# A hybrid GLA/MLA layer on one core: the two output-gate projections of GLA as one seven-product scheme on token tiles, between the two v projections

## The chip, the cores and the metric

The kernel runs on one core of a Trainium2 chip. The metric is the device time of one launch in microseconds (us). The kernel before takes 894.04 us, the median of three runs (893.48 to 894.49). One more execution was taken with the hardware profiler; every time below is from that one unless it is called a median of runs.

## The reference, cut to what matters

One decoder layer on 512 tokens with a model width of 1024, all in fp32. It has two sub-layers: token mixing (gated linear attention, GLA, and latent attention, MLA, side by side on the same normalised input, merged by gates) and a squared-ReLU MLP. The change touches the GLA branch.

```python
h = layer_norm(x, ln_in_g, ln_in_b)                      # 512 x 1024
q_g, k_g, v_g, r_g, a_lr, q_lat, kv_lat, gate_logits = split(h @ w_in)
log_a = log_sigmoid(a_lr @ w_gla_a2 + b_gla_a2) / 16     # decay of each key channel
o_gla = gla_chunked(q_g * 128 ** -0.5, k_g, v_g, log_a)  # 4 heads, dk 128, dv 256
o_gla = rms_norm(o_gla, gla_norm_g)                      # per head
y_gla = (o_gla * silu(r_g)) @ w_o_gla
y_mla = ...                                              # latent attention
g_gla, g_mla = split(sigmoid(gate_logits + b_gate))
mix = (g_gla * y_gla + g_mla * y_mla) @ w_out
```

`r_g` is 512 tokens x 1024 columns: 256 columns for each of four heads. Only `silu(r_g)` is used, and only by the last step of a head's output. The product that makes it, `h @ w_in[:, r]`, is what the change computes in another way.

## The kernel before: tiles, stages and who sets the order

**Products.** An fp32 product is made of three fp32r matmuls. `split` (L109) makes a high part on ACT (a copy) and a low part on DVE (a subtraction); the three matmuls are high by high, high by low and low by high, summed in PSUM. `hT` holds the normalised input as eight tiles of 128 channels x 512 tokens, each in a high and a low part.

**Weights.** `plan` (L144) puts pieces of 512 KB (two blocks of 128 rows x 512 columns) on a list, the stream. `pump` (L177) asks for the piece after next from DRAM (`fetch`, L163, on SP's queue, into one of three `wraw` buffers) and splits the next piece into `whi` on ACT (L189) and `wlo` on DVE (L190). `whi` and `wlo` have two buffers each.

**Two ways to lay out a product.** `gemm_fm` (L235) puts output columns on the partitions and tokens along the free axis. `gemm_tm` (L260) puts tokens on the partitions: for each of eight blocks of 128 rows and each of four token tiles it issues the three matmuls of L279 to L281, each 128x512, so that 512 output columns take 8 x 4 x 3 = 96 of them in four PSUM banks. v and r use `gemm_tm`, in two halves of 512 columns (two heads) each.

**Order of the work.** A Python program writes the instructions; each engine runs its own in a fixed order that is set when the program is built. Side work is written as generators ("lanes"). `tick` advances the first `WID` lanes by one step (to their next `yield`) from inside a product's loop, and `finish` drives a lane to its end at once. So where a `tick` stands decides between which matmuls a lane's instructions land; a scheduler at build time may still shift instructions of different lanes against each other.

The stages around the change, in time: the latents, q and k (k until about 93 us), then `proj_v(0)` (heads 0 and 1), `proj_r(0)`, `finish(t_lat2)`, `proj_v(1)` (heads 2 and 3), `proj_r(1)` (until about 225 us), then the first gate product g,0 and the seven-product units g0 and g1.

**Lanes that run there.** `lane_levels` runs `gla_levels` (L667) for head 0, 1, 2, 3. For each block size s from 2 to 256 POOL advances running sums of the decay (`advance`, L680 and L681), ACT takes exponentials (L686), DVE multiplies them with q and k (`M`, L688), PE makes the scores (L742), and DVE puts them into the score tile `SD` (L698, L733, L734), or splits them (s128, s256). `proj_v(1)` drives this lane through head 1 before it copies its results out. `lane_out` runs `gla_out` (L765) for each head once its scores, its v and its gate r are there: PE multiplies scores by v (L785 to L787), ACT squares and sums (L789, `osq`), DVE scales (L792, `gss`), POOL takes the power -0.5 (L794, `grs`), DVE multiplies by the gate (L799, `og`), PE transposes (L805).

`proj_r` copies each PSUM bank out by a tanh on ACT (L654, `th`) and two DVE operations (L658, `rg`).

**Sums of h.** The units g0 and g1 already use a seven-product scheme (a form of Winograd's and Strassen's) on 2 x 2 blocks of weight and input. They need sums of quarters of `hT`. `h_early` (L944) forms them on DVE (L949 to L956), splits them (128x512, `sh`) and stores them to DRAM (`hsd`), as a lane spawned after the q product; `h_load` (L1111) loads them again. `u_load` (L1031) forms a sum of weights by transfers alone: one load into a `wq` tile from SP's queue and one accumulating transfer onto it from POOL's (L1036). `unit` (L1038) calls `tick(3)` after every second of its four row blocks. After g0's product "t3" the program runs `finish(*t_gla)`.

## Time and profile before

| what | value |
|---|---|
| median of three runs | 894.04 us (893.48 to 894.49) |
| profiled execution | 894.09 us |
| its span on the core | 892.3 us |
| granted TensorE clock, mean | 0.997 |
| PE busy | 875.2 us, 98% |
| DVE busy | 619.0 us, 69% |
| ACT busy | 459.4 us, 51% |
| POOL busy | 168.0 us, 19% |
| DMA | 119.38 MB, mean 134 GB/s |

PE is the matrix engine, PEld its weight loads, DVE the vector engine, ACT the scalar engine, POOL the GpSimd engine; SP issues most of the transfers. A row of a timeline gives the start, the duration, the engine, the line of the kernel, the operation, output and inputs, and in brackets how long the engine stood idle before it and what ended that. A row of waits gives the waiting instruction, what ended its waits, the sum in us, how many, and the longest. A row of groups gives, after the bar, busy time and mean ns of one, and after the second bar the idle time before. Matmuls are pipelined: the duration of one (0.39 us for 128x512) overlaps the next.

### The profile page before, as it was taken

What the parts mean: (1) busy time and instruction counts of PE and PEld (TensorE: products, weight loads), DVE (VectorE), ACT (ScalarE), POOL (GpSimd) and SP (SyncE); (2) the same over time, 40 slices, a digit from 0 to 9 for tenths busy, and PEclk for the clock granted to TensorE, in tenths of its full rate; (3) what the DMA queues carried; (4) which work ended last, traced back from release to release, by engine and by line L of the source; (5) the groups of instructions that cost most, each with busy time, mean ns of one, the idle gap of its engine ahead of it and who ended that gap; (6) DMA issues with size and microseconds to landing.
All of it is one profiled execution on the core that took longest, in us unless ns stands there. A gap on an engine that the chain in (4) does not pass through costs nothing.

```text
span 892.3 us, 12880 instructions
## 1 busy us (share of the span) xinstructions
PE 875.2 (98%) x4868; PEld 762.5 (85%) x4868; DVE 619.0 (69%) x1002; ACT 459.4 (51%) x808; POOL 168.0 (19%) x192
## 2 busy tenths in 40 slices
PE   6999999999999999999999999999999999999996
PEld 5988888888899988888888888988888888889985
DVE  7838987568365745657756797887556646787865
ACT  6456554455365543445644424365457546656720
POOL 1003555436120010100000002003500520131000
PEclk9999999999999999999999999999999999999998
DMA  7416632212997423121207618005950990399312
GB/s 247 121 47 200 225 119 72 71 48 68 305 272 195 124 89 112 38 60 54 96 24 273 197 48 306 2 1 122 308 136 9 273 257 29 79 230 235 118 65 79
DMA packets 80254, 119.38 MB, mean 134 GB/s; under 512 B 8464, under 2 KB 46224, under 8 KB 80192
## 3 DMA queue, kind: packets, MB, share of 16 engines
q1 hardware_dynamic: 63680, 85.54, 30.0%
q0 software_dynamic: 14592, 29.37, 14.7%
q10 hardware_dynamic: 1920, 3.66, 1.1%
q8 instruction: 38, 0.62, 0.3%
q14 instruction: 24, 0.20, 0.1%
HBM read 97.04 MB, written 8.91 MB: 119 GB/s over the span
## 4 chain that ended last, share of the span: by engine, by line
PE 94%; DVE 3%; DMA 1%; issue 1%; ACT 0%; POOLq 0%; DVEq 0%
PE mm L245 12%; PE mm L247 12%; PE mm L246 12%; PE mm L279 7%; PE mm L280 7%; PE mm L281 7%; PE mm L1061 3%; PE mm L1060 3%; PE mm L1059 3%; PE px L1344 2%; PE px L1345 2%; PE px L1343 2%; PE mm L1344 2%; PE mm L1345 2%; PE mm L1343 2%; PE px L742 2%
## 5 line engine op out<-in xcount | busy, mean ns | idle before, releaser
L190 DVE TENSOR_TENSOR wlo<-wraw,whi 128x1024 fp32r<-128x1024 f32 (+2 forms) x95 | 105.4, 1109 | 108.4 <-ACT whi L189 103.9
L189 ACT ACTIVATE whi<-wraw 128x1024 fp32r<-128x1024 f32 (+2 forms) x95 | 90.7, 955 | 89.5 <-PE mm L246 36.6
L245 PE MATMUL mm<-h,whi 128*128 128x512 f32 x256 | 99.9, 391 | 0.0
L246 PE MATMUL mm<-h,whi 128*128 128x512 f32 x256 | 99.9, 390 | 0.0
L247 PE MATMUL mm<-h,wlo 128*128 128x512 f32 x256 | 95.5, 389 | 0.0
L1362 POOL DMA_DIRECT2D res<-ev x42 | 37.3, 1008 | 179.0 <-ACT ev L1360 154.7
L190 DVE TENSOR_TENSOR wlo<-wq,whi 128x1024 fp32r<-128x1024 f32 x36 | 44.1, 1225 | 27.0 <-ACT whi L189 26.8
L247 PEld LDWEIGHTS mm<-h,wlo 128*128 128x128 f32 x256 | 48.1, 188 | 10.0
L245 PEld LDWEIGHTS mm<-h,whi 128*128 128x128 f32 x256 | 48.1, 188 | 9.7
L246 PEld LDWEIGHTS mm<-h,whi 128*128 128x128 f32 x256 | 48.1, 188 | 9.6
L189 ACT ACTIVATE whi<-wq 128x1024 fp32r<-128x1024 f32 x36 | 38.1, 1058 | 26.2 <-PE mm L1060 14.3
L279 PE MATMUL mm<-whi,h 128*128 128x512 f32 x128 | 50.7, 409 | 0.0
L280 PE MATMUL mm<-wlo,h 128*128 128x512 f32 x128 | 50.5, 395 | 0.0
L281 PE MATMUL mm<-whi,h 128*128 128x512 f32 x128 | 50.2, 394 | 0.0
L1060 PE MATMUL mm<-sh,whi 128*128 128x256 f32 x160 | 45.3, 283 | 0.0
L1059 PE MATMUL mm<-sh,whi 128*128 128x256 f32 x160 | 45.3, 283 | 0.0
L1061 PE MATMUL mm<-sh,wlo 128*128 128x256 f32 x160 | 45.3, 283 | 0.0
L189 ACT ACTIVATE xh<-wraw 128x1024 fp32r<-128x1024 f32 (+1 forms) x28 | 27.4, 987 | 29.2 <-PE mm L281 15.9
L190 DVE TENSOR_TENSOR xl<-wraw,xh 128x1024 fp32r<-128x1024 f32 (+1 forms) x28 | 31.3, 1130 | 9.6 <-ACT xh L189 9.5
L686 ACT ACTIVATE E<-rp 128x256 f32<-128x256 f32 x64 | 26.1, 417 | 22.7 <-POOL rp L681 13.9
L1405 ACT ACTIVATE relu<-mm 128x512 f32<-128x512 f32 x24 | 14.1, 596 | 41.8 <-PE mm L247 41.8
L409 POOL TENSOR_TENSOR mv<-mv,mhalf 128x1 f32<-128x1 f32 x4 | 3.3, 837 | 170.3 <-DVE mv L408 170.3
(433 smaller groups left out, 2662.8 us busy)
## 6 DMA issues: line engine op xcount, KB each, us to landing
wraw<-in_w_ff_dram SPq DMA_DIRECT2D x36, 512.0 KB, 5.2
wraw<-in_w_in_dram SPq DMA_DIRECT2D x35, 512.0 KB, 3.5
wq<-in_w_ff_dram POOLq DMA_DIRECT2D x26, 512.0 KB, 9.5
res<-ev POOLq DMA_DIRECT2D x42, 256.0 KB, 9.8
wq<-in_w_in_dram SPq DMA_DIRECT2D x10, 512.0 KB, 5.5
hsd<-sh SPq DMA_DIRECT2D x16, 256.0 KB, 2.6
sh<-hsd SPq DMA_DIRECT2D x16, 256.0 KB, 5.3
wraw<-in_w_o_gla_dram SPq DMA_DIRECT2D x8, 512.0 KB, 3.7
```

The costliest lines, as they stand in the source:

```text
L189: st["ins"] = act(hi[:, :nk, :n], raw[:, :nk, :n], AF.Copy)
L190: st["lo"] = vtt(lo[:, :nk, :n], raw[:, :nk, :n], f(hi[:, :nk, :n]), op=ALU.subtract)
L245: mm(o, hi[:, c], xh, start=first, stop=False)
L246: mm(o, hi[:, c], xl, start=False, stop=False)
L247: mm(o, lo[:, c], xh, start=False, stop=last)
L279: mm(o, xh, hi[:, :n], start=opens, stop=False, skip_group_check=share)
L280: mm(o, xh, lo[:, :n], start=False, stop=False, skip_group_check=share)
L281: mm(o, xl, hi[:, :n], start=False, stop=last, skip_group_check=share)
L1059: mm(oa, hi[:, k, c], xh, start=opens and k == 0 and a == 0, stop=False, skip_group_check=True)
L1060: mm(oa, hi[:, k, c], xl, start=False, stop=False, skip_group_check=True)
L1061: mm(oa, lo[:, k, c], xh, start=False, stop=k == 3, skip_group_check=True)
L1362: nc.gpsimd.dma_start(res[tt + t][:, j * T:(j + 1) * T], e, accum_op=ALU.add)
```

## The change

Both halves of r become one product in seven parts. The 1024 rows of the weight are paired in blocks of 128 (even and odd), the 1024 columns are halves of 512, and the tokens are halves of 256. The seven products are, in this order, "11", "21", "t2", "t1", "t3", "22" and "t4". Each multiplies one weight block, or a sum of blocks, with one quarter of `hT`, or a sum of quarters, over four row blocks and two token tiles: 4 x 2 x 3 = 24 matmuls of 128x512. Products accumulate in the same PSUM bank where the scheme allows it; six banks are also copied to SBUF (`er`) and combined there by DVE. `silu` is the former evacuation.

The t weights are sums made by transfers: `r_prep`, a new lane, loads the block "12" three times (twice 512 KB each, SP's queue) and adds "11" or "22" to it by accumulating transfers from POOL's queue (t2 gets both); after the product "t1", `r_acc4` adds "21" onto t2's tile, which makes t4. The sums of `hT` come from `h_early`'s DRAM tiles, loaded by `x_load` from SP's queue. `h_early` therefore starts before q (after six empty steps), splits by 256 columns and stores four tiles for each pair of blocks; both lanes are finished before `proj_r`.

The order is now v for heads 0 and 1, all of r, v for heads 2 and 3. The gates of heads 2 and 3 are complete one product before those of heads 0 and 1, and `gla_out` waits until all four token tiles of its head's gate are there. In g0, the tick after the second row block is gone, and `finish(*t_gla)` follows "t4" in place of "t3".

```diff
@@ -302,15 +302,34 @@
         PL["lat", i] = plan("w_in", C_A + i * half, half, res=True)
     PL["q"] = plan("w_in", C_Q, T)
     PL["k"] = plan("w_in", C_K, T)
-    for hp in range(2):
-        PL["v", hp] = plan("w_in", C_V + hp * T, T)
-        PL["r", hp] = plan("w_in", C_R + hp * T, T)
+    WQ = {}
+
+    RY, RT, RA4 = 2, ((0, 0), (1, 0), (1, 1)), "t1"
+    RW = (("11", 0), ("21", 1), ("t2", 3), ("t1", 2), ("t3", 6), ("22", 5), ("t4", 4))
+
+    def r_src(op, hf):
+        i, j = int(op[0]) - 1, int(op[1]) - 1
+        c0 = C_R + j * T
+        return I["w_in"].rearrange("(k p) n -> p k n", p=P)[:, 4 * hf + i:4 * hf + i + 3:2, c0:c0 + T]
+
+    PL["v", 0] = plan("w_in", C_V, T)
+    PL["r"] = []
+    for op, _ in RW:
+        for hf in range(2):
+            PL["r"].append(len(stream))
+            e = {"nk": 2, "n": T, "res": False}
+            if op[0] == "t":
+                e["src"] = lambda q=("r", op, hf): WQ[q]
+            else:
+                e["dmas"] = [(slice(0, 2), r_src(op, hf), None)]
+            stream.append(e)
+    PL["v", 1] = plan("w_in", C_V + T, T)
+
...
@@ -646,18 +665,94 @@
...
-    def proj_r(hp):
-        hs = (2 * hp, 2 * hp + 1)
-
-        def e(a, j, ps):
-            th = B([P, T], F32, "th")
-            act(th, ps, AF.Tanh, scale=0.5)
-            for i, h in enumerate(hs):
-                if Rg[h] is None:
-                    Rg[h] = A([P, NT, HV], F32, "rg")
-                stt(Rg[h][:, a, :], th[:, i * HV:(i + 1) * HV], 1.0, ps[:, i * HV:(i + 1) * HV],
-                    op0=ALU.add, op1=ALU.mult)
-        gemm_tm([PL["r", hp]], hT, T, e, fine=3)
+    def silu(j, a, ps):
+        th = B([P, T], F32, "th")
+        act(th, ps, AF.Tanh, scale=0.5)
+        for i in range(2):
+            h = 2 * j + i
+            if Rg[h] is None:
+                Rg[h] = A([P, NT, HV], F32, "rg")
+            stt(Rg[h][:, a, :], th[:, i * HV:(i + 1) * HV], 1.0, ps[:, i * HV:(i + 1) * HV],
+                op0=ALU.add, op1=ALU.mult)
+            rgn[h] += 1
+
+    rgn = [0] * GH
+
+    def r_acc(to, op):
+        for hf in range(2):
+            nc.gpsimd.dma_start(WQ["r", to, hf], r_src(op, hf), accum_op=ALU.add)
+
+    def r_load(to):
+        for hf in range(2):
+            t = WQ["r", to, hf] = A([P, 2, T], F32, "wq")
+            nc.sync.dma_start(t, r_src("12", hf))
+
+    def r_prep():
+        for step in (lambda: r_load("t2"), lambda: r_acc("t2", "11"), lambda: r_load("t1"), lambda: r_acc("t2", "22"),
+                     lambda: r_load("t3"), lambda: r_acc("t1", "11"), lambda: r_acc("t3", "22")):
+            step()
+            for _ in range(RY):
+                yield
+
+    def proj_r():
+        bank, e, xs = {}, {}, {}
+
+        def x_load(ph):
+            xs[ph] = []
+            for p in range(4):
+                t = B([P, 2, 256], F32R, "xr")
+                nc.sync.dma_start(f(t), hsd[p][(2, 3, 5, 6).index(ph)])
+                xs[ph].append((t[:, 0], t[:, 1]))
+
+        nat = {0: (0, 0), 1: (1, 0), 4: (1, 1)}
+        for n, (op, ph) in enumerate(RW):
+            if n + 1 < len(RW) and RW[n + 1][1] not in nat:
+                x_load(RW[n + 1][1])
+            if ph in nat:
+                i, h = nat[ph]
+                x = [tuple(hT[2 * p + i][:, w, 256 * h:256 * h + 256] for w in range(2)) for p in range(4)]
+            else:
+                x = xs.pop(ph)
+            opens = ph in (0, 1, 2)
+            for hf in range(2):
+                it = PL["r"][2 * n + hf]
+                pump(it)
+                hi, lo = stream[it]["w"]
+                for pp in range(2):
+                    xh, xl = x[2 * hf + pp]
+                    for t in range(2):
+                        key = ("a" if ph in (0, 3, 6, 4) else "b", t)
+                        if ph in (0, 1) and not hf and not pp:
+                            bank[key] = MM()
+                        o, c = bank[key], slice(t * P, (t + 1) * P)
+                        mm(o, xh[:, c], hi[:, pp], start=opens and not hf and not pp, stop=False, skip_group_check=True)
+                        mm(o, xh[:, c], lo[:, pp], start=False, stop=False, skip_group_check=True)
+                        mm(o, xl[:, c], hi[:, pp], start=False, stop=hf == 1 and pp == 1, skip_group_check=True)
+                    if (hf, pp) in RT:
+                        tick(None)
+            for t in range(2):
+                a, b = bank["a", t], bank.get(("b", t))
+                if ph in (0, 3, 2):
+                    e[ph, t] = B([P, T], F32, "er")
+                    act(e[ph, t], b if ph == 2 else a, AF.Copy)
+                elif ph == 1:
+                    vtt(e[0, t], b, e[0, t], op=ALU.add)
+                    silu(0, t, e[0, t])
+                elif ph == 6:
+                    vtt(e[2, t], e[2, t], a, op=ALU.subtract)
+                    silu(1, 2 + t, e[2, t])
+                elif ph == 5:
+                    vtt(e[3, t], b, e[3, t], op=ALU.subtract)
+                    silu(1, t, e[3, t])
+                else:
+                    silu(0, 2 + t, a)
+            if op == RA4:
+                r_acc4()
+
+    def r_acc4():
+        for hf in range(2):
+            WQ["r", "t4", hf] = WQ["r", "t2", hf]
+        r_acc("t4", "21")
 
     SS = [None] * GH
 
@@ -763,7 +858,7 @@
         yield
 
     def gla_out(h):
-        while SS[h] is None or Vh[h] is None or Rg[h] is None:
+        while SS[h] is None or Vh[h] is None or rgn[h] < NT:
             yield
         sd, s128, s256 = SS[h]
 
@@ -942,6 +1037,8 @@
     hsd = []
 
     def h_early():
+        for _ in range(6):
+            yield
         for p in range(4):
             raw = [B([P, T], F32, "hraw") for _ in range(2)]
             for i in range(2):
@@ -955,12 +1052,12 @@
             vtt(X[1][:, 0], a12, X[0][:, 1], op=ALU.add)
             vtt(X[1][:, 1], a11, a21, op=ALU.subtract)
             yield
-            for x in X:
-                xs = [B([P, 2, 256], F32R, "sh") for _ in range(2)]
-                split(x, *xs)
-                hsd.append([DR([P, 2, 256], "hsd") for _ in range(2)])
-                for t, d in zip(xs, hsd[-1]):
-                    nc.sync.dma_start(d, f(t))
+            hsd.append([DR([P, 2, 256], "hsd") for _ in range(4)])
+            for i, x in enumerate(X):
+                xs = [B([P, 2, 256], F32R, "hs") for _ in range(2)]
+                for e in range(2):
+                    split(x[:, e], xs[e][:, 0], xs[e][:, 1])
+                    nc.sync.dma_start(hsd[p][2 * i + e], f(xs[e]))
                 yield
 
     t_ln1 = spawn(ln_in1())
@@ -972,9 +1069,10 @@
...
     t_lat = spawn(latents())
+    t_he = spawn(h_early())
     gemm_fm(PL["q"], hT, T, ev_q)
     t_lat2 = spawn(latents2())
-    t_he = spawn(h_early())
+    t_rp = spawn(r_prep())
     gemm_fm(PL["k"], hT, T, ev_k)
     finish(t_prep, t_lat)
     lv = [False] * GH
@@ -996,10 +1094,10 @@
 
     WID[0] = 3
     proj_v(0)
-    proj_r(0)
+    finish(t_he, t_rp)
+    proj_r()
     finish(t_lat2)
     proj_v(1, lambda: levels_upto(1))
-    proj_r(1)
     t_gla = [t_lv, t_out]
 
 
@@ -1059,7 +1157,7 @@
                         mm(oa, hi[:, k, c], xh, start=opens and k == 0 and a == 0, stop=False, skip_group_check=True)
                         mm(oa, hi[:, k, c], xl, start=False, stop=False, skip_group_check=True)
                         mm(oa, lo[:, k, c], xh, start=False, stop=k == 3, skip_group_check=True)
-                    if k % 2:
+                    if k == 3 or k == 1 and key != "g0":
                         tick(3)
                 if ph == 0:
                     e1[g] = B([P, T], F32, "e1")
@@ -1113,15 +1211,13 @@
...
-            for i in range(2):
-                xh, xl = [B([P, 2, 256], F32R, "sh") for _ in range(2)]
-                for t, d in zip((xh, xl), hsd[2 * p + i]):
-                    nc.sync.dma_start(f(t), d)
-                o[(2, 5)[i]], o[(3, 6)[i]] = (xh[:, 0], xl[:, 0]), (xh[:, 1], xl[:, 1])
+            for x, ph in enumerate((2, 3, 5, 6)):
+                t = B([P, 2, 256], F32R, "sh")
+                nc.sync.dma_start(f(t), hsd[p][x])
+                o[ph] = (t[:, 0], t[:, 1])
             hops.append(o)
             yield
 
-    finish(t_he)
     spawn(h_load())
     u_load("g0", "t1")
     u_load("g0", "22")
@@ -1145,7 +1241,7 @@
     prods = {"g0": unit("g0", hops, ev_gate0, after0), "g1": unit("g1", hops, ev_gate, after)}
     for key, op in GATES:
         prods[key](op)
-        if op == "t3" and key == "g0":
+        if op == "t4" and key == "g0":
             finish(*t_gla)
     hT = hops = None
 
```

More of the change, by code (lines that the diff above doesn't have):

```diff
@@ L311, in tile_hybrid_block @@
     PL["g", 0] = plan("w_in", C_G, T)
-    WQ = {}
     HOME = {"w": ("whi", "wlo"), "r": ("wraw", "wraw"), "a": ("xh", "xl")}
```

## The prediction

> **What bounds the kernel now.** I read the page first (busy shares, then the chain that ended last), next the busy time by stage, then PE's own waits, and at last the timelines of POOL, DVE and ACT around the r and v products.
>
> ```profile
> span 892.3 us, 12880 instructions
> PE 875.2 (98%) x4868; PEld 762.5 (85%) x4868; DVE 619.0 (69%) x1002; ACT 459.4 (51%) x808; POOL 168.0 (19%) x192
> PE 94%; DVE 3%; DMA 1%; issue 1%; ACT 0%; POOLq 0%; DVEq 0%
> ```
> ```profile
> core 0: us, PE busy (x) PEld busy (x) DVE busy (x) ACT busy (x) POOL busy (x), PEclk, DMA share, GB/s
> 91.00:128.00 37.00, 36.02 (x196) 30.40 (x195) 36.31 (x66) 22.06 (x47) 19.55 (x24) 1.00 0.51 173
> 128.00:160.00 32.00, 32.00 (x177) 27.37 (x177) 23.16 (x40) 15.48 (x33) 17.45 (x19) 1.00 0.23 68
> 160.00:194.00 34.00, 34.00 (x201) 29.74 (x200) 21.19 (x38) 17.30 (x46) 15.20 (x17) 1.00 0.21 65
> 194.00:225.00 31.00, 31.00 (x186) 27.20 (x184) 22.46 (x43) 17.64 (x37) 17.02 (x19) 1.00 0.27 85
> 225.00:262.00 37.00, 37.00 (x224) 32.97 (x223) 15.65 (x23) 14.82 (x31) 7.42 (x6) 1.00 1.03 285
> ```
> PE is the only bound. The five windows are, in order, the first v product, the first r product, the second v, the second r, and gate 0 with the start of the seven-product units. PE is busy without a gap in the last four, at the full clock (the column 1.00 before the DMA share). The first is the odd one: DVE 36.31 of 37 us, PE 36.02. Its PE waits are these two, of all between 90 and 262:
>
> ```profile
> PE px L742 <- DVE SD L734: 0.7, 1, 0.7
> PE px L746 <- DVE M L688: 0.2, 1, 0.2
> ```
> So a PE instruction taken out pays its whole price, as long as no new wait opens; and any wait that does open on PE is paid in full. The sum is made against the profiled execution, 894.09 us (span 892.3 and 1.8 around it), which stands 0.05 us above the median, 894.04.
>
> **The count of matmuls.** Both r halves are 2 x 96 = 192 matmuls of 128x512. Seven products of 24 are 168. One such matmul costs its distance to the next one, not its pipelined duration:
>
> ```profile
> 95.95 0.39 PE L279 MATMUL mm<-whi,h 128*128 128x512 f32 x1
> 96.17 0.39 PE L280 MATMUL mm<-wlo,h 128*128 128x512 f32 x1
> 96.40 0.39 PE L281 MATMUL mm<-whi,h 128*128 128x512 f32 x1
> 96.63 0.39 PE L279 MATMUL mm<-whi,h 128*128 128x512 f32 x1
> ```
> Three in 0.68 us, 0.227 each: 24 x 0.227 = 5.45 us off PE. No other PE work changes in number.
>
> **Moving the sums of h (h_early) from k and v0 forward into q and k.** Its sums, splits and stores leave the one stretch where DVE is full, so I take the 0.7 + 0.2 = 0.9 us of PE waits there as gone (bounds 0 and 0.9). It now splits by 256 columns: 16 pairs in place of 8.
>
> ```profile
> 68.64 1.23 DVE L190 TENSOR_TENSOR wlo<-wraw,whi 128x1024 fp32r<-128x1024 f32 x1 [6.57 <-ACT whi L189]
> 91.16 2.73 DVE L527 COPY qk<-mm 128x512 f32<-128x512 f32 x4 [0.39 <-PE mm L247]
> L112 DVE TENSOR_TENSOR sh<-hx,sh 128x512 fp32r<-128x512 f32 x4 | 3.6, 892 | 0.0
> ```
> By these, a 256-column split on DVE is at least half of 0.892, so the cost is 0 to a few us of DVE time, covered by idle like the 6.57 us during q. Without that cover the k evacuations (2.73 us) would come late, and with them the banks that v0 opens with; the built order does put h_early work and the transposes of krh closer to them. I charge 0.4 us (0 to 1).
>
> **The weight sums: SP and POOL.** Six 512 KB loads go to SP's queue and eight accumulating transfers to POOL's, woven between the advances (L680, L681) of head 0's level chain during v0; two more follow the t1 product.
>
> ```profile
> 94.38 1.70 POOL L680 TENSOR_TENSOR rp<-rp 128x256 f32<-128x256 f32 x1 [8.44 <-DVE rp L671]
> 117.12 1.03 POOL L680 TENSOR_TENSOR rp<-rp 128x256 f32<-128x256 f32 x1 [5.29 <-ACT E L686]
> 120.28 0.95 POOL L681 TENSOR_TENSOR rp<-rp 128x256 f32<-128x256 f32 x1
> ```
> ```profile
> L1036 POOL DMA_DIRECT2D wq<-in_w_in_dram x6: 1283/1298/1481, 225.7 to 268.3; - x6
> DMA to landing us min/median/max: 5.9/10.1/15.9
> POOL wq L1036 <- DMA wq<-in_w_in_dram: 15.6, 3, 12.2
> 251.64 1.32 POOL L1036 DMA_DIRECT2D wq<-in_w_in_dram  x1 [12.25 <-DMA wq<-in_w_in_dram]
> L1288 POOL DMA_DIRECT2D wq<-in_w_ff_dram x24: 712/736/1034, 539.8 to 706.5; - x24
> ```
> ```profile
> 123.83 1.61 DVE L112 TENSOR_TENSOR vl<-mm,vh 128x256 fp32r<-128x256 f32 x4
> 125.54 0.58 PE L279 MATMUL mm<-whi,h 128*128 128x512 f32 x1
> ```
> The chain of head 0 took 94.38 to 121.23, 26.9 us, and POOL stood idle in it for 5.29 us in one piece and some 3 us in small ones. POOL's engine time for an accumulating issue is 1.30 us (L1036, the same operation on the same weights), against 0.74 for the issues of L1288, of the same size. Eight cost 10.4 us, or 5.9. The 5.29 us of idle stood behind ACT and DVE work that includes h_early and can be filled; of the rest about 1.3 us can. So the chain ends 10.4 - 6.6 = 3.8 us later at the first price, and 0.7 earlier at the second. Behind its last levels, in DVE's order, stand the vl evacuations of v0 (123.83); PE opens the next product at 125.54, and needs the bank that the first of them (two heads, 0.8 us) frees at 124.6, about 1 us of slack. With what DVE no longer does, PE would stand for some 2 us at the first price and 0 at the second. I take 1.0, between them, as an estimate; bounds 0 and 5.5 (the latter if POOL also waits a few us for a load). If the SP loads land late, an accumulate waits in POOL's queue and head 0's remaining advances wait behind it, as the 12.25 us at 251.64 shows. The two accumulates after t1 stand likewise ahead of head 1's advances.
>
> By the Trainium skill, page "DMA: Bandwidth & Descriptors", section "Anatomy of one DMA — SWDGE (gpsimd) path", a transfer from POOL's queue takes about 2.0 us plus its bytes over 436 GB/s, an estimate of 3.2 us for 512 KB; the trace disagrees, with 5.9 to 15.9 for the accumulating ones, and the measurement decides. By that figure no second addition would be waited for, and the sum would stand nearer the case in which all is hidden.
>
> **Inside the seven products.**
>
> ```profile
> L189 ACT ACTIVATE whi<-wraw 128x1024 fp32r<-128x1024 f32 x20 | 21.1, 1057 | 15.9 <-PE mm L246 4.4 <-DMA hsd<-sh 4.4 <-issue 3.3
> L190 DVE TENSOR_TENSOR wlo<-wraw,whi 128x1024 fp32r<-128x1024 f32 x21 | 27.1, 1292 | 13.7 <-ACT whi L189 13.7
> L654 ACT ACTIVATE th<-mm 128x512 f32<-128x512 f32 x8 | 4.7, 592 | 2.2 <-PE mm L281 2.0
> ```
> Fourteen weight pieces are split in place of eight: 6 x 1.06 = 6.3 us more on ACT, 6 x 1.29 = 7.8 on DVE; six copies of banks to SBUF at the price of tanh, 6 x 0.59 = 3.6 on ACT; six additions on DVE, priced by half a split (same 128x512), 6 x 0.65 = 3.9. DVE gets 11.7 us more and ACT 9.9 in the stretch 128 to 225, where they were busy 66.8 and 50.4 of 97 us. That is room on the mean; but a product of 24 matmuls lasts 5.4 us, its two splits take 2.6 of DVE, and where level work and an evacuation fall into the same product little is left. I charge 0.5 us (0 to 2). The sixteen reloads of h sums (256 KB, SP) and the net 12 more weight transfers have room from 128 to 194 (DMA share 0.21 to 0.23); if they are late, the t products wait for xr.
>
> **Order of the gates and of gla_out.** Heads 2 and 3 get their gates first and heads 0 and 1 with the last product, so head 0's output waits for the whole of r, then runs in v1, head 1's in gate 0, and heads 2 and 3 in g0, where ticks now come once a product. v1 is charged nothing: its cover is the PE-full 31 us of matmuls; without it up to 1. At g0's start a weight split (1.06) and a state copy stand ahead of the tanh of gate 0 on ACT, which frees a bank: 0.4 (0 to 1.1). Inside g0 the built order has head 2's last L787 product only 8 matmuls of 128x256 ahead of the transposes of its result. That loop in the kernel before, for head 3:
>
> ```profile
> 256.59 0.28 PE L787 MATMUL px<-vh,sd 128*128 128x256 f32 x1
> 256.71 0.28 PE L1059 MATMUL mm<-sh,whi 128*128 128x256 f32 x1
> 256.91 0.38 ACT L789 ACTIVATE osq<-px 128x256 f32<-128x256 f32 x1 [0.86 <-PE px L787]
> 257.42 0.17 DVE L792 TENSOR_SCALAR gss<-gss 128x4 f32<-128x4 f32 x1
> 257.68 1.03 POOL L794 TENSOR_TENSOR grs<-gss,mhalf 128x4 f32<-128x4 f32 x1 [1.78 <-DVE gss L792]
> 258.74 1.27 DVE L799 SCALAR_TENSOR_TENSOR og<-px,grs,rg 128x256 f32<-128x256 f32 x3 [1.15 <-POOL grs L794]
> 259.37 0.30 PE L805 MATMUL px<-ca,og 128*128 128x128 f32 x1
> ```
> From the product to the transpose it takes 259.37 - 256.59 = 2.78 us; 8 matmuls cover 8 x 0.12 = 0.96. PE stands for 1.8 us (bounds 0, if PE comes there late for another reason and the result is ready, and 2.8, if POOL's reciprocal root also queues behind an accumulate of g0's weights).
>
> **Sum.** -5.45 - 0.9 + 0.4 + 1.0 + 0.5 + 0.4 + 1.8 = -2.25 us: 894.09 - 2.25 = 891.8. By the bounds alone it lies between -6.35 and -5.45 + 13.4 = +7.95.
>
> **Rivals.** *All new waits are hidden:* POOL pays 0.74 an issue and the loop in g0 costs nothing. -5.45 - 0.9 = -6.35, 887.7 us. For it: PE's waits in this stage were 0.9 us in 172. Against it: the 2.78 us loop over 0.96 of cover is plain in the order. *The scheme pays for itself and no more:* each charge stands at some 1.8 times mine (v0's 2.0, the products 2.0), +7.5 in place of +4.1, so 895.2, or down to a gain under 1.8 us. For it: DVE splits of 1.29 in products of 5.4 us; against: DVE's third of idle time there. *Slower: POOL's queue blocks on a load.* One accumulate in v0 waits 12.25 us, as at 251.64; 5.29 fits into the old idle, so head 0's chain ends 7.0 + 3.8 us later and PE stands for 10.8 - 1.3 = 9.5 in place of 1.0: -2.25 + 8.5 = +6.2, 900.3. It decides from a stall of about 5 us. For it: seven 512 KB loads issued close together where 173 GB/s flow already, and 285 was the rate of the stretch with DMA share 1.03; against: h_early's stores have left that stretch, and plain loads land in some 5 us:
>
> ```profile
> wq<-in_w_in_dram SPq DMA_DIRECT2D x10, 512.0 KB, 5.5
> ```
> *Also slower: DVE keeps POOL from issuing.* If every accumulate in v0 waits for one DVE split of 1.22 us (as at 68.64), POOL carries 8 x 1.22 = 9.8 us more, PE stands for 12 in place of 1: 903. Against it: six issues of L1036 spread only from 1283 to 1481 ns, with DVE busy about half the time.
>
> That last case is a rule of the Trainium skill, "SBUF — State Buffer", section "SBUF: two separate sides": a DVE operation that holds both ports locks out POOL, which then cannot write the descriptors of its transfers. No row of L1036 here shows a lockout of that length.
>
> **How the numbers follow.** 0.2% is 1.8 us, about what a measurement of this kernel can tell from no change. The forecast case (a gain of 1.8 to 4) has 0.35, all hidden 0.18, pays only for itself 0.25, POOL blocked on a load 0.18, locked out by DVE 0.04. Faster: 0.35 + 0.18 = 0.53; same: 0.25; slower: 0.22. The range runs from 888.0, next to the hidden case, to 898.0, which leaves out the longer half of the blocked cases and the lockout; the likeliest case alone is 890.0 to 892.3.
>
> **What would show it.** Matmuls 24 fewer, PE busy down by about 5.5. PE's waits from 90 to 265: one at v0's end on a bank that vl frees (1 us), one on og before L805's counterpart in g0 (1.8 us). POOL's accumulates near 1.30 us each, with waits on the wq loads of a few us at most in v0. The prediction is wrong if POOL shows a wait of 8 us or more there, or if the r products show PE waiting for wlo, xr or er by more than 2 us in all.

## The result, and the profile after

The changed kernel takes 900.29 us (median of four runs, 899.98 to 900.7) against 893.76 (893.3 to 894.49) of the kernel before: 1.0073 times as long, 95% interval 1.0055 to 1.009. That is 6.5 us slower; the forecast was 891.8, 2.25 us under the profiled execution of the kernel before, and the range ended at 898.0. The profiled execution took 900.7 us.

The page of the changed kernel, the span, the busy times and the queue of POOL's transfers:

```profile
span 898.6 us, 12965 instructions
PE 874.0 (97%) x4844; PEld 758.1 (84%) x4844; DVE 629.8 (70%) x1022; ACT 467.7 (52%) x828; POOL 183.0 (20%) x202
q0 software_dynamic: 17312, 34.61, 17.8%
```
The 24 matmuls are gone (4868 to 4844), yet PE's busy time fell by 1.2 us only, and 6.3 us were added to the span. By stage, with the columns as in the windows of before (PE first, granted clock, DMA share and GB/s last):

```profile
91.00:128.00 37.00, 34.09 (x182) 28.90 (x181) 28.71 (x54) 19.27 (x41) 26.88 (x29) 0.99 1.07 301
128.00:160.00 32.00, 29.27 (x136) 22.76 (x136) 24.51 (x35) 17.74 (x35) 16.28 (x17) 0.96 0.96 269
```
The first v product now leaves PE idle for 2.9 us instead of 1.0, and the first r products, where PE had no gap before, for 2.7. DVE is *less* busy in v0 than before (28.71 against 36.31). What rose is the share of the DMA engines: from 0.51 to 1.07 and from 0.23 to 0.96. PE's waits (the waiting instruction, what ended the wait, us in all, times, longest):

```profile
PE mm L729 <- DVE wlo L190: 1.8, 3, 0.7
PE mm L728 <- DVE vl L112: 1.7, 1, 1.7
PE px L900 <- DVE og L894: 1.6, 1, 1.6
PE px L637 <- ACT krh L631: 1.2, 1, 1.2
PE mm L728 <- ACT whi L189: 0.6, 1, 0.6
PE mm L280 <- DVE wlo L190: 0.5, 1, 0.5
```
To place every lost microsecond, the start-to-start distance of each pair of matmuls was compared with the usual distance of that shape (0.227 us for 128x512), from 92 us to the end of g0. The kernel before loses 5.2 us this way, the changed one 16.3. The losses over 0.3 us of the changed kernel, and its stretch at half clock, are in this table. The rest is small pieces, 5.0 us in the changed kernel and 3.8 in the kernel before, beside that one's two waits.

| at us | PE stands for | lost us |
|---|---|---|
| 94.4 | krh transposes, ahead of the first v product | 1.36 |
| 124.5 | first product of r, a bank that vl frees | 1.88 |
| 127.0 to 130.4 | granted clock 0.5 | 1.5 |
| 135 to 141 | weights of product "21" (whi 0.90, wlo 0.69 and 0.70) | 2.29 |
| 150 to 152 | M (0.47) and wlo of t1 (0.89) | 1.36 |
| 174.7, 184.7 | x of a level (0.43), wlo of v1 (0.69) | 1.12 |
| 259.3 | og in g0 | 1.76 |

The balance: 16.3 - 5.2 = 11.1, less 5.45 for the matmuls, is 5.65. Another 0.65 had come before the last matmul of k, 0.5 of it ahead of the very first matmul; together this is the 6.3 of the span.

The weights of "21" were late because their transfers were. The transfers issued from 95 to 140 us, per queue (packets, MB, share of 16 engines) and per group (count, KB each, median us from issue to landing), first the kernel before, then the changed one:

```profile
q1 hardware_dynamic: 2806, 5.78, 38.8%
wraw<-in_w_in_dram SPq DMA_DIRECT2D x6, 512.0 KB, 3.5
```
```profile
q1 hardware_dynamic: 4463, 9.00, 57.3%
q0 software_dynamic: 2176, 4.19, 50.3%
wq<-in_w_in_dram POOLq DMA_DIRECT2D x8, 512.0 KB, 19.3
wraw<-in_w_in_dram SPq DMA_DIRECT2D x6, 512.0 KB, 16.6
```
A piece of weights took 3.5 us before and 16.6 now. The times of the packets add up to more than the whole stretch on all engines (57.3% + 50.3%). ACT meets the two late pieces here:

```profile
135.16 1.06 ACT L189 ACTIVATE whi<-wraw 128x1024 fp32r<-128x1024 f32 x1 [2.20 <-DMA wraw<-in_w_in_dram]
138.86 1.06 ACT L189 ACTIVATE whi<-wraw 128x1024 fp32r<-128x1024 f32 x1 [1.68 <-DMA wraw<-in_w_in_dram]
```
POOL's queue, on which the prediction laid the weight, waits for loads 6.5 us in all, at most 3.4:

```profile
L683 POOL DMA_DIRECT2D wq<-in_w_in_dram x10: 1192/1258/1672, 98.9 to 146.5; - x10
DMA to landing us min/median/max: 7.1/17.2/23.2
POOL wq L683 <- DMA wq<-in_w_in_dram: 6.5, 3, 3.4
```

### The profile page after: what moved, and what is told of

Read it like the earlier page. It is cut to its first block, busy times and chain, and to the rows that moved or that the text cites. A ratio compares the mean times of both kernels' runs of the same rounds, so it can differ in the third digit from the quotient of the medians.

```text
span 898.6 us, 12965 instructions
## 1 busy us (share of the span) xinstructions
PE 874.0 (97%) x4844; PEld 758.1 (84%) x4844; DVE 629.8 (70%) x1022; ACT 467.7 (52%) x828; POOL 183.0 (20%) x202
## 4 chain that ended last, share of the span: by engine, by line
PE 87%; DVE 5%; DMA 4%; ACT 1%; POOL 1%; issue 1%; POOLq 0%; SPq 0%; DVEq 0%; ACTq 0%
PE mm L245 11%; PE mm L247 11%; PE mm L246 11%; PE mm L281 5%; PE mm L280 5%; PE mm L279 5%; PE mm L1159 3%; PE mm L1158 3%; PE mm L1157 3%; PE px L1441 2%; PE px L1439 2%; PE px L1440 2%; DMA wraw<-in_w_in_dram 2%; PE mm L1441 2%; PE mm L1439 2%; PE mm L1440 2%
## 5 line engine op out<-in xcount | busy, mean ns | idle before, releaser
L190 DVE TENSOR_TENSOR wlo<-wraw,whi 128x1024 fp32r<-128x1024 f32 (+2 forms) x93 | 101.7, 1094 | 110.2 <-ACT whi L189 105.6
L189 ACT ACTIVATE whi<-wraw 128x1024 fp32r<-128x1024 f32 (+2 forms) x93 | 88.5, 952 | 95.1 <-PE mm L246 34.1
L190 DVE TENSOR_TENSOR wlo<-wq,whi 128x1024 fp32r<-128x1024 f32 x44 | 54.3, 1234 | 24.8 <-ACT whi L189 24.8
L189 ACT ACTIVATE whi<-wq 128x1024 fp32r<-128x1024 f32 x44 | 46.5, 1057 | 25.1 <-PE mm L1158 10.5
L783 DVE TENSOR_TENSOR M<-E,qk 128x512 f32<-128x512 f32 x32 | 28.4, 892 | 11.7 <-ACT E L781 11.7
L775 POOL TENSOR_TENSOR rp<-rp 128x256 f32<-128x256 f32 x32 | 29.2, 912 | 33.5 <-ACT E L781 24.2
L776 POOL TENSOR_TENSOR rp<-rp 128x256 f32<-128x256 f32 x32 | 32.1, 1004 | 4.6 <-ACT q L806 2.3
## 6 DMA issues: line engine op xcount, KB each, us to landing
res<-ev POOLq DMA_DIRECT2D x42, 256.0 KB, 10.1
```

What stands on the lines that cost most here:

```text
L189: st["ins"] = act(hi[:, :nk, :n], raw[:, :nk, :n], AF.Copy)
L190: st["lo"] = vtt(lo[:, :nk, :n], raw[:, :nk, :n], f(hi[:, :nk, :n]), op=ALU.subtract)
```

## The experiments

Theory A: the accumulating transfers fill the DMA engines and so delay the weight pieces. Theory B: POOL's time for issuing them, and the order of its queue, delay head 0's levels. Theory C: DVE and ACT are too full inside the products. Theory D came later: the lane of `r_prep` displaces other lanes. The changed kernel was measured only in the first group of runs, so a difference to its 900.29 us also holds what moved between the groups; the kernel before, run in each group, had medians from 893.65 to 893.93.

**Bytes away, instructions kept.** PE and DVE run the same instructions in the same order; seven places of POOL's order, six of ACT's and two of SP's differ. The kernel leaves out 31 of 32 columns of each addition.

```diff
-            nc.gpsimd.dma_start(WQ["r", to, hf], r_src(op, hf), accum_op=ALU.add)
+            nc.gpsimd.dma_start(WQ["r", to, hf][:, :, 0:16], r_src(op, hf)[:, :, 0:16], accum_op=ALU.add)
```


> The ten accumulating transfers of r's weight sums move 16 of their 512 columns, so 1/32 of the bytes, with the same instructions in the same order on every engine; the sums are then wrong outside these columns (left out: 31/32 of the weight sums). Theory A (the accumulating transfers fill the DMA engines: in the changed kernel they land about 4 us apart from 109 to 139 us while the weight pieces of the second product land 20 us after their issue instead of 3.5): pieces land in 3.5 to 6 us, PE's waits on the weights of product 21 (0.9 + 0.7 + 0.7 us) go, and if the late end of head 0's levels also comes from accumulates that wait for slow loads, part of the 1.9 us wait on vl and of the 1.4 us at half clock behind it: 896 to 898 us. Theory B (the issue time of the accumulates on POOL, 1.2 us each, and the order of its queue): POOL keeps its ten issues, the wait on vl stays, 899 to 900.3. Theory C (DVE and ACT are too full in the products): no change, 900.3.

Measured 894.83 us, 1.0013 times before (1.0003 to 1.0022): 5.5 us faster than the changed kernel. From 95 to 140 us:

```profile
q0 software_dynamic: 2176, 0.13, 9.0%
wraw<-in_w_in_dram SPq DMA_DIRECT2D x7, 512.0 KB, 5.4
```
```profile
L683 POOL DMA_DIRECT2D wq<-in_w_in_dram x10: 1198/1288/2160, 99.4 to 141.0; - x10
```
POOL still spends 1.29 us on each issue. The waits on product "21" are gone, and the one on vl is 1.2 us. B and C do not explain 5.5 us; A does. The gain is larger than A's range (896 to 898), since the loss at half clock (1.5) vanished too.

**Bytes kept, nothing added.** Here the order is the same on every engine; the sums are left out.

```diff
-            nc.gpsimd.dma_start(WQ["r", to, hf], r_src(op, hf), accum_op=ALU.add)
+            nc.gpsimd.dma_start(WQ["r", to, hf], r_src(op, hf))
```


> The ten accumulating transfers become plain ones of the same size from the same queue (the sums are left out: the tile keeps the last block loaded); same instructions, same order. Theory A in the form that an accumulate costs the DMA engines more than a load of its size: they land 1.5 to 2.5 us apart in place of 4, pieces of product 21 are less late, 897 to 899. If bytes alone count, 900. Theory B: each issue falls from 1.2 to about 0.74 us on POOL, 8 x 0.46 = 3.7 us less ahead of head 0's last levels: the wait on vl (1.9 + 1.4 us) goes, 897; C: no change.

Measured 894.39 us, ratio 1.0008 (0.9995 to 1.002): 5.9 us faster than the changed kernel with the same bytes moved. From 95 to 140 us:

```profile
q1 hardware_dynamic: 5616, 11.16, 69.4%
q0 software_dynamic: 1152, 4.19, 23.6%
wq<-in_w_in_dram POOLq DMA_DIRECT2D x9, 512.0 KB, 9.0
wraw<-in_w_in_dram SPq DMA_DIRECT2D x7, 512.0 KB, 8.8
```
Here is the price that was missing. The same 4.19 MB take 23.6% of the engines for 45 us as plain transfers and 50.3% as accumulating ones, with 1152 and 2176 packets: about 1.3 and 2.8 us of all sixteen engines for 512 KB. Theory A holds in the form "an accumulate costs twice a load of its size"; the form "bytes alone count" falls. Issuing is cheaper for a plain transfer as well (0.72 us), and the wait on vl is 0.4 here against 1.2 with the narrow sums: so B has a part, under a microsecond. The measured time is below every range that was expected (897 to 900.3).

The price is not one of smaller packets. In the packets of the traces, 95 to 140 us, one of 2048 bytes took 176 ns (median) in POOL's queue of the changed kernel and 84 ns in SP's; the plain transfers of this run went in packets of 4096 bytes, 159 ns each.

By the Trainium skill, page "Collectives: The Full Stack", section "The bandwidth ceiling: the fold count and why AG ≠ RS ≠ AR", the add of a ReduceScatter needs two source reads, both on the same ring, and so twice the reading traffic. The page speaks of collectives; the 2.1 times of these two runs (50.3% against 23.6%) agrees with it, but no run here shows the two reads themselves.

**The tick in g0 put back.**

```diff
-                    if k == 3 or k == 1 and key != "g0":
+                    if k % 2:
                         tick(3)
```


> The tick after the second row block of g0's products is put back; all else as changed. The transposes of head 2's result then stand further behind its last product, the wait of 1.76 us on og goes: 898.5. If another wait takes its place in g0 (heads 2 and 3 still end there), no change, 900.3.

Measured 902.74 us, ratio 1.01 (1.0085 to 1.0115): a miss. The wait on og stayed at 1.6 us and one of 1.0 us on osq joined it. Upstream, where instructions stand as in the changed kernel, this profile shows the clock at half twice and a 2.0 us wait on whi, so not all of the 2.4 us is the tick's.

**Two of the four sums moved into r.**

```diff
-        for step in (lambda: r_load("t2"), lambda: r_acc("t2", "11"), lambda: r_load("t1"), lambda: r_acc("t2", "22"),
-                     lambda: r_load("t3"), lambda: r_acc("t1", "11"), lambda: r_acc("t3", "22")):
+        for step in (lambda: r_load("t2"), lambda: r_acc("t2", "11"), lambda: r_acc("t2", "22")):
...
+            if op in ("11", "21"):
+                r_load({"11": "t1", "21": "t3"}[op])
+                r_acc(*{"11": ("t1", "11"), "21": ("t3", "22")}[op])
```


> The loads and sums of t1 and t3 are issued after the products 11 and 21 in place of during v0; t2's stay. Output complete. Theory A: half of the burst (two of four sums) leaves v0, pieces of product 21 land under 8 us after issue, PE's 2.3 us of waits there go, and head 0's levels end earlier: 896 to 897.5, unless the t1 sums now land after they are needed. Theory B: POOL has four accumulates fewer in v0, 4.8 us less: the wait on vl goes (3.3 us with the half clock), but head 1's levels get them: 897 to 899. Theory C: 900.

Measured 905.15 us, ratio 1.0126 (1.011 to 1.0142): the worst of all, outside every expectation; the reservation in A came true, for t3. Pieces of weights do land sooner in v0 (4 to 10 us), but the transfers' price is only moved, into r, beside the reloads of h sums, and t3's sums come too late. Waits of POOL, then the split of t3's second half on ACT:

```profile
POOL wq L683 <- DMA wq<-in_w_in_dram: 11.5, 2, 7.1
```
```profile
165.32 1.06 ACT L189 ACTIVATE whi<-wq 128x1024 fp32r<-128x1024 f32 x1 [2.33 <-DMA wq<-in_w_in_dram]
```
The 7.1 us are t2's second addition, which waits in POOL's queue for the first to land, with head 0's advances behind it: here the mechanism of the rival "POOL's queue blocks" is seen, and PE's wait on vl is 2.4 us.

**All sums issued from q on, beside the lanes.** The profile of the changed kernel has the DMA engines busy for 1 to 18% from 40 to 70 us.

```diff
+        for g in list(extra):        # in tick, after the lanes
+            if next(g, 1):
+                extra.remove(g)
...
-    RY, RT, RA4 = 2, ...
+    RY, RT, RA4 = 3, ...
+    extra.append(r_prep())
     gemm_fm(PL["q"], hT, T, ev_q)
     t_lat2 = spawn(latents2())
-    t_rp = spawn(r_prep())
```


> The same loads and accumulating transfers, issued from the start of the q product on with three ticks between steps, so that most of them run from 48 to 90 us, where the DMA engines are busy 1 to 18% of the time up to 70 us; output complete. Theory A (the accumulating transfers cost the DMA engines twice a plain one, and do harm where they meet a queue of weight pieces that PE waits for): weight pieces of product 21 land in 4 to 6 us, POOL's queue is free of six of eight accumulates during head 0's levels, both waits go (2.3 + 3.3 us): 893.5 to 895. Rival: the same harm moves to the pieces of q and k, which then land 10 us late: 897 or more, with PE waits on whi or wlo between 48 and 93 us.

Measured 891.51 us, ratio 0.9976 (0.9967 to 0.9985): 8.8 us faster than the changed kernel, faster than the kernel before, and below the range expected: the wait on krh, which that did not count, went too. Two things changed at once here, the place of the transfers and the lane that issues them; the version "late sums, own lane" below parts them. The weights of "21" are no longer late, nor do the waits on vl, krh and og exist. The scheduler placed the transposes of krh inside the first v product here, as in the kernel before.

**Fewer sums.** One tile becomes t1, t2 and t4 in turn.

```diff
-    RW = (("11", 0), ("21", 1), ("t2", 3), ("t1", 2), ("t3", 6), ("22", 5), ("t4", 4))
+    RW = (("11", 0), ("21", 1), ("t1", 2), ("22", 5), ("t2", 3), ("t3", 6), ("t4", 4))
...
+            if op in ("t1", "t2"):
+                to, add = {"t1": ("t2", "22"), "t2": ("t4", "21")}[op]
+                for hf in range(2):
+                    WQ["r", to, hf] = WQ["r", op, hf]
+                r_acc(to, add)
```


> Order 11, 21, t1, 22, t2, t3, t4, with one tile that becomes t1, then t2 (plus 22), then t4 (plus 21): four loads and four accumulates before r in place of six and eight, four accumulates inside r; output complete. Theory A: the burst in v0 halves; if the waits on product 21 and on vl scale with it, 896 to 898; the sums inside r land 6 to 9 us after issue and have about 8 us. If they are late, ACT waits for wq in r and it is 899 to 901.

Measured 899.61 us, ratio 1.0066 (1.0051 to 1.0081): inside the range expected for late sums, but not for that reason. The waits on "21" and vl are gone, but two new ones take their place:

```profile
PE mm L727 <- DVE er L741: 2.9, 1, 2.9
PE px L834 <- DVE M L780: 2.6, 2, 2.3
```
Neither ACT nor DVE waits for a transfer in r, so the sums were not late. With this order the combination of banks on DVE ends too late for the next product, and DVE's M of a level comes late behind the work of the products (evacuations and splits). The clock also stood at half for 6.8 us from 146.9 us on.

**krh held back.**

```diff
+        yield
         p = PX(dt=F32R)
-        for tt in range(NT):
-            nc.tensor.transpose(...krh...)
+        with tc.issue_after(st["mm"].ins):
+            for tt in range(NT):
+                nc.tensor.transpose(...krh...)
```


> The transposes of the rotated keys (krh) are held behind matmuls of the first v product, as they stood in the kernel before; else as changed. PE's wait of 1.36 us ahead of the first v product goes: 899.0. If the wait only hid another one (k's last evacuations free the banks just then), 900.3.

Measured 899.81 us, ratio 1.0075 (1.006 to 1.009): by the ratio no difference from the changed kernel, where 1.3 us were expected. PE now waits 0.9 us at the same place, at the first matmul of v0:

```profile
94.65 2.47 DVE L546 COPY qk<-mm 128x512 f32<-128x512 f32 x4
95.47 0.47 PE L279 MATMUL mm<-whi,h 128*128 128x512 f32 x1 [0.90 <-ACT krh L631]
```
The profile puts the wait down to krh's copy on ACT, which ended at 95.35. But that matmul does not read krh, and its weights had been split by 93.15; what it needs is the first PSUM bank that DVE's evacuation of k frees (`qk`, the first of the four copies ends at 95.33). So the other expectation fits: the wait on krh had hidden one on k's banks. The order behind it shifted as well, with a 2.2 us wait on M and one of 1.8 us on a reload of h sums.

**og held back in g0.**

```diff
+        if h == 2:
+            yield
+            yield
...
+                if h == 2:
+                    gates.enter_context(tc.issue_after(st["um"].ins))
```


> In g0 the transposes of head 2's result are held behind a later product (about 32 matmuls of 128x256, 3.8 us, in place of 8, after its last matmul); else as changed. The 1.76 us wait on og goes: 898.6. If head 3's part then ends late in g0, 900.3 or more.

Measured 899.26 us, ratio 1.0057 (1.004 to 1.0074): 1.0 us faster than the changed kernel, though the two intervals overlap. The wait on og is gone, and 0.5 us of others came in g0. So the term was real; from 230 us to the end of g0 PE loses 1.4 us here and 2.6 in the changed kernel.

**The early sums without spacing, and closer together.** In the early version, RY = 0 (all at once, at the start of q) and RY = 2.

> As the early version (891.5), but all six loads and eight sums are issued at once at the start of q, with no ticks between; matmuls, DVE and ACT in the same order as there. Theory A (an accumulating transfer keeps the DMA engines busy twice as long as a plain one: 50.3% against 23.6% of 45 us for the same 4.19 MB): eight cost 23 us of all engines and six loads 8, which fits between 41 and 75 us, but q's pieces in that stretch land 8 to 15 us after issue; with about 10 us of lead PE waits 0 to 4 us in q: 891.5 to 895. If place alone matters and not spacing, 891.5.

> As the early version (891.5) with two ticks between steps in place of three: the last sums end some 15 us earlier, further from head 0's levels. Theory A: 891 to 891.5. If the sums then meet the stores of h and the latents (80 to 95 us) more closely, 892.

Measured 891.19 us (ratio 0.9969, 0.9959 to 0.998) and 892.19 (0.9983, 0.9974 to 0.9992). Of the burst, the transfers issued from 38 to 75 us and PE's waits from 46 us to the end of g0:

```profile
q0 software_dynamic: 2176, 4.19, 62.1%
wq<-in_w_in_dram POOLq DMA_DIRECT2D x8, 512.0 KB, 13.9
wraw<-in_w_in_dram SPq DMA_DIRECT2D x3, 512.0 KB, 7.2
```
```profile
PE px L842 <- DVE M L788: 1.6, 3, 1.0
PE px L846 <- DVE M L788: 0.3, 1, 0.3
PE mm L734 <- DVE wlo L190: 0.3, 1, 0.3
```
Two of q's pieces take 7 to 8 us, which its lead covers; PE waits for nothing in q. The burst is 2.6 us under the kernel before. Place matters most. Spacing counts for less, but not for nothing: with RY = 2 every run (891.77 to 892.93) is slower than every run of the burst (890.73 to 891.68), as the second expectation had it (892). Its profile places only 0.3 us of the 1.0, a wait on the latents at 81 us, where its sums still run. Between the burst and the early version (891.51) the intervals overlap.

**h_early alone, on the kernel before.** Spawned ahead of q, six empty steps, splits by 256 columns; r as before.

> The kernel before with h_early alone moved ahead of q and split by 256 columns; r stays two products of 96 matmuls each, in the old order. The prediction's step: 0.9 us of PE waits in the first v product go, 0.4 us come at its start: 893.3. If the wait of 1.36 us on krh in the changed kernel comes from this move (DVE full from 80 to 100 us), 894.5 to 895.

Measured 894.00 us, ratio 1.0004 (0.9994 to 1.0013): no difference. Its PE waits over q, k, v and r:

```profile
PE px L742 <- DVE M L688: 0.5, 2, 0.3
```
The wait on krh is not there, so this move alone does not cause it.

**Late sums, own lane.** As the early version, but `r_prep` starts with the first v product (RY = 1), so its transfers fall into v0 as in the changed kernel.

> The changed kernel with r_prep stepped beside the lanes, not as one of the three that a tick advances, from the start of the first v product, so that its transfers stay in v0 as changed while head 0's levels keep their place in the lanes. Theory A (the transfers' cost on the DMA engines in v0): product 21's pieces are still late, 896 to 898.5. Theory D (the lane order that r_prep changed, which delays levels and krh): 891.5 to 893, as the early version. Both in part: after to here is the lanes' share, here to 891.5 the transfers' share of the 8.8 us between the two.

Measured 897.83 us, ratio 1.0049 (1.0033 to 1.0066): inside A's range, and 2.5 us under the changed kernel. From 95 to 140 us, and PE's waits:

```profile
q0 software_dynamic: 2176, 4.19, 50.3%
wq<-in_w_in_dram POOLq DMA_DIRECT2D x8, 512.0 KB, 14.0
wraw<-in_w_in_dram SPq DMA_DIRECT2D x7, 512.0 KB, 7.9
```
```profile
PE px L642 <- ACT krh L636: 2.7, 1, 2.7
PE mm L734 <- DVE wlo L190: 1.5, 4, 0.7
PE px L842 <- DVE M L788: 0.9, 2, 0.6
```
From the changed kernel to here 2.5 us: lanes, and a spread of the transfers that came with it. From here to the burst in q 6.6 us, with the place of the transfers changed and the matmuls' order adapted by the scheduler. The 2.7 us wait on krh among these is another matter: it comes from POOL, where two steps of `kr`, a memset and an accumulate (1.29 us as a rule) all stretch, while DVE works without a pause until 105.74.

```profile
101.17 4.74 POOL L528 TENSOR_TENSOR kr<-kt,kt 128x64 f32<-128x64 f32 x1
101.68 5.65 POOL L688 DMA_DIRECT2D wq<-in_w_in_dram  x1
104.53 1.21 DVE L190 TENSOR_TENSOR wlo<-wraw,whi 128x1024 fp32r<-128x1024 f32 x1
```
It looks like the rival in which DVE keeps POOL from issuing; no run tests it, and the cause stays open. So the 6.6 us are not the transfers' alone. Their cleanest measure is the 5.9 us of the plain transfers, where not one instruction changed place.

## Why the prediction was wrong, point by point

**The count of matmuls: right.** In the burst version PE loses 7.5 us to gaps between 46 us and the end of g0, in the kernel with h_early alone 4.7; 7.5 - 4.7 - 5.45 = -2.65, and between these two kernels 891.19 - 894.00 = -2.8 was measured. The 5.45 us are there; in the changed kernel 11.1 us of new gaps cover them.

**The weight sums: the step that failed.** The prediction priced an accumulate by POOL's issue time (1.30 us by 8, on head 0's chain) and took 1.0 us, bounds 0 to 5.5. POOL's issues did cost what it said (1.26 us median), and the chain of head 0 ran from 99.94 to 126.1 us, 26.1 us long against 26.9: the idle pieces swallowed them. It only began 5.6 us later, since DVE's copy of the decay (L766, at 99.35) stood behind other lanes' work; in the two versions with `r_prep` beside the lanes it began at 95.0 and 95.1. But the price on the DMA engines stood nowhere in the sum. The prediction looked for room in 128 to 194 us (share 0.21 to 0.23), and counted 12 more transfers of weights where there are 14 (22 in place of 8). Most of them fall into v0, where 0.51 were taken already and 23 us of engine time for eight sums and about 8 for six loads had to fit into 45. What the runs showed in its place is 5.9 us between accumulating and plain transfers of the same size and order, of which POOL's shorter issues have a part under a microsecond. The trace of before held the hint: its six accumulates landed after a median of 10.1 us, plain loads into the same tiles after 5.5, and from 225 to 275 us a packet of 1024 bytes took 102 ns in POOL's queue and 46 ns in SP's.

The whole miss is 8.5 us. The 2.6 that the plain transfers leave are other terms, those at v0's start and in the products below among them, and not all of them were placed.

**The rival with the right number had the wrong place.** "POOL's queue blocks on a load" gave 900.3, and 900.29 was measured; but POOL's longest wait was 3.4 us, not 12.25. The number itself was luck: the working spends POOL's 5.29 us of idle time twice, once on the issues (10.4 - 6.6 = 3.8) and once on the wait (12.25 - 5.29 = 7.0); counted once, the rival would have stood near 905.6. The delayed pieces were SP's, which needed 16.6 us. What spoke for that rival, loads issued close together into a stretch at 173 GB/s, pointed at the right stretch. But the loads alone do no such harm: with the same six loads and eight plain transfers beside them the time was 894.39. The lockout of POOL by DVE did not happen in the changed kernel, where ten issues spread from 1192 to 1672 ns; one issue of 5.65 us in the late-sums version may have been one.

**The wait on vl: named, mis-sized.** Forecast 1.0, measured 1.88, and 1.5 more at half clock behind it; with plain transfers 0.4.

**h_early: -0.9 and +0.4, together -0.5.** Alone it makes no measurable difference (+0.2 us, interval of the ratio around 1). In the changed kernel 1.36 us are lost at v0's start, more than the bound of 1, at the place and in the way that the prediction named: k's evacuations on DVE start at 94.82 in place of 91.16, behind h_early's work, and krh's transposes, which the built order now puts ahead of v0, wait for copies on ACT that end at 95.83.

```profile
93.62 1.28 DVE L1046 TENSOR_TENSOR hraw<-h 128x512 f32<-128x512 f32 x2
94.82 1.88 DVE L546 COPY qk<-mm 128x512 f32<-128x512 f32 x3
95.11 0.72 ACT L631 ACTIVATE krh<-kr 128x256 fp32r<-128x256 f32 x2 [5.68 <-POOL kr L523]
```
It takes `r_prep` as one of the three lanes as well: in the late-sums version, with `r_prep` beside the lanes, the evacuations start at 91.86 and v0 at 94.50, without a wait. Why the scheduler orders the lanes in this way was not tried.

**Inside the products: 0.5.** With plain transfers PE waits 0.6 us in r (0.3 on wlo, 0.3 on x): about right. Another 0.5 on wlo falls into v1, which was charged nothing. In the changed kernel 4.8 us, of which 2.3 are late pieces.

**g0: 0.4 at its start, 1.8 in it.** Nothing at the start; 1.76 in it, at the place and for the reason given. It was the best term of the sum.

## What to carry to other kernels

The price of an accumulating transfer does not show in its bytes or in the instruction that issues it: here it kept the DMA engines busy 2.1 times as long as a plain one, and the harm appeared in another queue, at weight pieces that took 16.6 us in place of 3.5. Before sums by transfers are put beside a stream of weights, add up the engine time of that stretch, at twice the price for accumulates, and put them where the DMA share is near zero, even nearly 90 us ahead of their use: that, with the lane that issues them kept out of the other lanes' turns, made 2.6 us gained out of 6.5 lost.

## What the runs showed of the hardware that was not expected

After the 1.72 us wait ahead of r, the granted clock fell to half while PE was busy again; each matmul of 128x512 then took 0.43 us in place of 0.227. Windows of the changed kernel (columns as above, the clock is the third from the end):

```profile
124.00:126.00 2.00, 0.69 (x8) 0.48 (x7) 1.93 (x5) 1.69 (x6) 1.84 (x3) 1.00 1.11 262
127.00:128.00 1.00, 1.00 (x4) 0.81 (x3) 0.93 (x3) 1.00 (x2) 0.00 (x0) 0.51 1.15 270
129.00:130.00 1.00, 1.00 (x4) 0.81 (x3) 1.00 (x4) 0.32 (x1) 0.00 (x0) 0.50 1.10 262
131.00:133.00 2.00, 2.00 (x14) 1.48 (x14) 0.43 (x1) 0.63 (x1) 0.00 (x0) 1.00 1.09 260
```
The half clock lasted 3.4 us, about 1.5 us of lost time, so a wait of 1.7 us cost nearly twice its length. It came once or twice in most versions with waits over a microsecond, and not in others. The late-sums version waited 2.7 us for krh and kept the full clock. The early version and its burst, with the same order of matmuls, both wait 1.0 us for M near 171 us; the first then ran at half clock from 174 to 178 us and the second did not. By the Trainium skill, page "TensorE: Matmul & The Clock Gate", section "What's actually happening", the clock falls after an idle window of about 3.4 us and the windows run freely; the 3.4 us length and the chance character agree, but here the idle pieces were 1.0 to 1.9 us long, shorter than such a window.
